# Re-ordering attention and batching the border columns in a scheduled two-layer backbone step on eight cores

## The chip, the cores and the metric

One Trainium2 chip, eight cores, one launch. The metric is the device time of the slowest core in microseconds. Each core works on its own data; the cores do not talk to each other. Executions come in two states: in the slow one, the cores of one die (0 to 3 or 4 to 7) have a lower granted clock and the time is some per cent longer. Profiles are of the slowest core, unless another core is named.

## The reference, cut to what matters

```python
D_MODEL = 1024; D_FF = 2816; SEQ = 256; DEC_SEQ = 2048; PAST_LEN = 512; N_HEADS = 8; N_KV_HEADS = 2

def dwconv3(x, w):                     # centred, width 3, over positions
    xp = jnp.pad(x, ((0, 0), (1, 1), (0, 0)))
    return xp[:, :-2] * w[0] + xp[:, 1:-1] * w[1] + xp[:, 2:] * w[2]

def short_conv_mixer(u, w_in, conv_k, w_out):
    b_gate, c_gate, xp = jnp.split(u @ w_in, 3, axis=-1)
    return (b_gate * dwconv3(c_gate * xp, conv_k)) @ w_out

def conv_ffn(u, w_up, conv_k, w_down):
    h = dwconv3(u @ w_up, conv_k)
    g, up = jnp.split(h, 2, axis=-1)
    return (jax.nn.silu(g) * up) @ w_down

for i in range(2):                     # for context (prompt) and latent tokens
    u = modulate_norm(h, norm_mix_pre[i], s1, sc1)
    y = short_conv_mixer(u, ...) if i == 0 else attention(u, ...)   # latents: rotary q/k, cached + own keys
    h = gated_residual(h, y, norm_mix_post[i], g1)                  # h + gate * rms_norm(y)
    u = modulate_norm(h, norm_ffn_pre[i], s2, sc2)
    h = gated_residual(h, conv_ffn(u, ...), norm_ffn_post[i], g2)
# ... the six modulation vectors come from silu(c) @ mod_w[i]; the prompt's new k, v are outputs too
```

Each core has one latent sequence of 2,048 tokens and four prompts of 256. The kernel cuts this into three units of 1,024 tokens: S0 and S1 (the halves of the latent sequence) and P (the four prompts).

## The kernel before

The program is not written in execution order. Every operation is registered with what it reads and writes; a list scheduler then simulates the engines with modelled durations and fixes one static order for each engine. Priorities are planned TensorE times. An operation that others depend on takes over their urgency; a DMA is wanted 12 us ahead of its first reader:

```python
for o in reversed(self.ops):
    for s in o.succ:
        o.prio = min(o.prio, s.prio - (12.0 if o.nbytes else 1.3 * o.lat))
```

Weights pass through a ring of 23 blocks of 1 KB in each partition. One channel of a ConvFFN's up-projection takes four blocks, so five channels fit; a block of the modulation weights takes four blocks as well:

```python
def load_w(src, cols, after=()):
    nb = (cols * 2 + 1023) // 1024
    if wpos["b"] + nb > wpos["lim"]:
        wpos["b"] = 0
    b = wpos["b"]
    wpos["b"] += nb
    # ...
    P.dma("pool", ap, src, cols * 2 * 128, reads=after, writes=keys)
```

The width-3 convolution needs the neighbour's column at the border of S0 and S1. Before each layer part, S0 gets that one column of S1's normed input (`uh`) and multiplies it with every weight tile ("halo" matmuls of one column). Later S1 reuses a saved column of S0. The result goes into the channel by a one-column VectorE update (`edge`), in the middle of the channel's own chain:

```python
def ffn_in(U, l, ub):                  # cut
    for c in range(NCF):               # 22 channels
        w, wk = load_w(wup[l, c], KC * 256)
        for s in range(2):
            b = nextset()
            o = ((c % 2) * 2 + s) * 1024
            r, rk = ev_t[:, o:o + 1024], A("ev", o * 4, o * 4 + 4096)
            zmm(b, ub, ..., wk, halo=s if U is S0 else None)   # L581, and L588: the halo
            z = z2(b)
            P.act(1024, ..., r, z, AF.Copy, scale=fck(1, s, c))
            if U is S0:
                edge(r, 1023, bank(7, 1, s), fck(2, s, c), ...)            # L610
            if U is S1:
                edge(r, 0, zc, fck(0, s, c), ...)                          # L610
            taps(U, r, z, fck(0, s, c), fck(2, s, c), ...)                 # L606, two per half
        # ... Silu, product into ra
```

`ev_t` is also where an output phase keeps its result until the residual has been added. The order of the stages is: three convolutions (S0, S1, P); FFN-0 (S0, S1, P); S0's and S1's projections; S0's attention; S1's; the prompt's projections and attention; FFN-1 (S0, S1, P). The residual h of two units stays on the chip; h is spilled and reloaded around every stage (72 stores and 72 loads of 512 KB).

Of the kernel before, what the change touches and what calls it, by code (L numbers as in the profile page):

```python
# [13 lines left out]
KC = 8  # L14
DFF = 2816
NCF = 22
# [23 lines left out]
class Prog:  # L40
# [75 lines left out]
    def schedule(self):  # L116
# [11 lines left out]
        for o in reversed(self.ops):  # L128
            for s in o.succ:
                o.prio = min(o.prio, s.prio - (12.0 if o.nbytes else 1.3 * o.lat))  # L130
        order = []
        n = len(self.ops)
        eps = 0.05
        while len(order) < n:
# [51 lines left out]
            for s in o.succ:  # L186
                lag = 0.0 if (s.eng == e == "pe") else 0.06
                s.ready = max(s.ready, (o.t0 + o.busy if s.eng == e == "pe" else o.t1) + lag)
                s.ndep -= 1
                if s.ndep == 0:  # L190
                    heapq.heappush(future[s.eng], (s.ready, s.idx))
# [55 lines left out]
def build_program():  # L247
# [26 lines left out]
    h_mem = nc.dram_tensor("h_mem", [128, KC, TT], F32, kind="Internal").ap()  # L274

    with ExitStack() as es:
# [25 lines left out]
        hc2_t = sb("hc2", 8 * 2 + 4, F32)  # L302
        hsq_t = sb("hsq", 8, BF16)
        uh_t = sb("uh", 8, BF16)
        zs_t = sb("zs", 44, F32)
        ps = es.enter_context(nc.psum_tensor("ps", [128, 4096], F32))[:]
# [25 lines left out]
        first = {"w": ()}  # L332
# [80 lines left out]
        class UBuf:  # L413

            def __init__(self, name, base, ap):
                self.name, self.base, self.ap = name, base, ap.rearrange("p (k t) -> p k t", k=KC)

# [7 lines left out]
        UK = UBuf("ra", 16384, ra_t[:, 8192:16384])  # L425

# [36 lines left out]
        def norm(U, l, ai, bpart, ub, bk=5, allpool=False):  # L463
            mv, cf = mvs[l], cfs[l]
            for ct in range(2):
# [13 lines left out]
                for kc in range(KC):  # L479
                    t = tm_t[:, (kc % 2) * 512:(kc % 2) * 512 + 512]  # L480
                    tk = [("tm", kc % 2)]
                    P.dve(lambda e, kc=kc, t=t, rs=rs, src=hap(U, kc, ct * 512, ct * 512 + 512): e.scalar_tensor_tensor(  # L482
                        out=t, in0=src, scalar=cf[:, ai, kc, U.v:U.v + 1], in1=rs,
                        op0=ALU.mult, op1=ALU.mult), 512, hk(U, kc, ct) + [("rs", ct), ("coef", l, ai, U.v)], tk)
                    P.dve(lambda e, kc=kc, t=t, ct=ct: e.tensor_scalar_add(
                        out=ub.ap[:, kc, ct * 512:ct * 512 + 512], in0=t, scalar1=mv[:, bpart * 8 + kc, U.v:U.v + 1]), 256,
                        tk + [("mod", l, bpart, U.v)], ub.keys(kc, ct * 512, ct * 512 + 512))

        def save_hcol():
            src = h_t[S1.slot].rearrange("p (k t) -> p k t", k=KC)[:, :, 0]  # L490
            P.dve(lambda e: e.tensor_copy(out=hcol_t, in_=src), 60, [k for kc in range(KC) for k in hk(S1, kc, 0)], [("hcol",)])

        def norm_halo(l, ai, bpart):
# [3 lines left out]
            ss, th = hc2_t[:, 16:17], hc2_t[:, 0:8]  # L497
# [9 lines left out]
        def out_phase(U, l, gi, nk, wsrc, rhs_fn, rkeys, ybs, banks, split=False):  # L507
# [4 lines left out]
            order = [(m, ct) for ct in range(2) for m in range(KC)] if split else [(m, ct) for m in range(KC) for ct in range(2)]  # L512

            def finish(ct):
                yb, ybn = ybs[ct]
                rs = rs_t[:, (2 + ct) * 512:(3 + ct) * 512]
                rk = [("rs", 2 + ct)]
                rstd_ops(6 + ct, 512, D, rs, rk)
                for m in range(KC):
                    y = yb[:, m * 512:(m + 1) * 512]  # L520
                    yk = A(ybn, m * 2048, m * 2048 + 2048)
                    P.dve(lambda e, y=y, m=m, rs=rs: e.scalar_tensor_tensor(  # L522
                        out=y, in0=y, scalar=cf[:, gi, m, U.v:U.v + 1], in1=rs, op0=ALU.mult, op1=ALU.mult), 512,
# [3 lines left out]
                    if split and ct == 1 and m % 2 == 0:  # L527
# [6 lines left out]
                    elif ct == 1:  # L534
                        store_h(U, m)

            for m, ct in order:
                yb, ybn = ybs[ct]
                if split or ct == 0:
                    w, wk = load_w(wsrc(m), nk * 128)  # L540
# [11 lines left out]
                y = yb[:, m * 512:(m + 1) * 512]  # L552
                yk = A(ybn, m * 2048, m * 2048 + 2048)
# [12 lines left out]
            if U is S1:  # L566
                save_hcol()
# [9 lines left out]
        def zmm(b, ub, lhs_fn, wk, halo=None):  # L577
# [7 lines left out]
            if halo is not None:  # L585
# [4 lines left out]
                P.pe(fh, 0.35, wk + [("uh",)], pk(7))  # L590
# [18 lines left out]
        def edge(r, col, zc, w, rd, wr):  # L609
            P.dve(lambda e: e.scalar_tensor_tensor(out=r[:, col:col + 1], in0=zc, scalar=w, in1=r[:, col:col + 1],  # L610
                                                   op0=ALU.mult, op1=ALU.add), 30, rd + wr, wr)

        def conv_in(U, ub):
            ck = lambda j, i: par[:, P_CK + j * 8 + i:P_CK + j * 8 + i + 1]
            for i in range(8):
                w, wk = load_w(win[i], KC * 384, after=first["w"])
                first["w"] = ()
                w3 = w.rearrange("p (k n) -> p k n", n=384)
                o = (i % 2) * 2048
                csb, ckk = ev_t[:, o:o + 1024], A("ev", o * 4, o * 4 + 4096)  # L620
                r, rk = ev_t[:, o + 1024:o + 2048], A("ev", o * 4 + 4096, o * 4 + 8192)
                bC = nextset()
                zmm(bC, ub, lambda kc, w3=w3: w3[:, kc, 128:256], wk, halo=0 if U is S0 else None)
                hc = hc2_t[:, 8 + i:9 + i]
                P.act(1024, "ps", pk(bC, bC + 1), ckk, csb, z2(bC), AF.Copy)
                if U is S0:
                    P.act(1, "ps", pk(7), [("hc", i)], hc, bank(7, 1, 0), AF.Copy)
                bX = nextset()
                zmm(bX, ub, lambda kc, w3=w3: w3[:, kc, 256:384], wk, halo=1 if U is S0 else None)
                P.dve(lambda e, csb=csb, bX=bX: e.tensor_tensor(out=csb, in0=csb, in1=z2(bX), op=ALU.mult), 1024,  # L630
                      pk(bX, bX + 1) + ckk, ckk)
                if U is S0:
                    P.dve(lambda e, hc=hc: e.tensor_tensor(out=hc, in0=hc, in1=bank(7, 1, 1), op=ALU.mult), 30,
                          pk(7) + [("hc", i)], [("hc", i)])
# [4 lines left out]
                if U is S0:  # L639
                    edge(r, 1023, hc, ck(2, i), [("hc", i), ("par",)], rk)  # L640
                    P.pool(lambda e, csb=csb, i=i: e.tensor_copy(out=zs_t[:, i:i + 1], in_=csb[:, 1023:1024]), 1, ckk, [("zs", i)])
                if U is S1:
                    edge(r, 0, zs_t[:, i:i + 1], ck(0, i), [("zs", i), ("par",)], rk)
                P.dve(lambda e, r=r, bB=bB, i=i: e.tensor_tensor(out=a3(i, 0, 1024), in0=r, in1=z2(bB), op=ALU.mult), 1024,
                      rk + pk(bB, bB + 1), a3k(i, 0, 1024))
                cur["k"] = a3k(i, 0, 1)
                yield

        def ffn_in(U, l, ub):
            fck = lambda j, s, c: par[:, P_FCK + l * 132 + j * 44 + s * 22 + c: P_FCK + l * 132 + j * 44 + s * 22 + c + 1]  # L650
            for c in range(NCF):
                w, wk = load_w(wup[l, c], KC * 256)
                w3 = w.rearrange("p (k n) -> p k n", n=256)
                rr = []
                for s in range(2):
                    b = nextset()
                    o = ((c % 2) * 2 + s) * 1024
                    r, rk = ev_t[:, o:o + 1024], A("ev", o * 4, o * 4 + 4096)
                    rr.append((r, rk))
                    zc = zs_t[:, c * 2 + s:c * 2 + s + 1]  # L660
                    zmm(b, ub, lambda kc, w3=w3, s=s: w3[:, kc, s * 128:(s + 1) * 128], wk, halo=s if U is S0 else None)
                    z = z2(b)
                    P.act(1024, "ps", pk(b, b + 1) + [("par",)], rk, r, z, AF.Copy, scale=fck(1, s, c))
                    if U is S0:
                        edge(r, 1023, bank(7, 1, s), fck(2, s, c), pk(7) + [("par",)], rk)
                    if U is S1:
                        edge(r, 0, zc, fck(0, s, c), [("zs", c * 2 + s), ("par",)], rk)
                    taps(U, r, z, fck(0, s, c), fck(2, s, c), pk(b, b + 1) + [("par",)], rk)
                    if U is S0:
                        P.act(1, "ps", pk(b + 1), [("zs", c * 2 + s)], zc, z[:, 1023:1024], AF.Copy)  # L670
                (rg, rgk), (ru, ruk) = rr
                P.act(1024, "sb", rgk, rgk, rg, rg, AF.Silu)
                P.pool(lambda e, rg=rg, ru=ru, c=c: e.tensor_tensor(out=a3(c, 0, 1024), in0=rg, in1=ru, op=ALU.mult), 1024,  # L673
                       rgk + ruk, a3k(c, 0, 1024))
                cur["k"] = a3k(c, 0, 1)
                yield

# [4 lines left out]
        ktp = ra_t[:, 18 * 1024:20 * 1024].rearrange("p (j s) -> p j s", j=2)  # L682
        vbp = ra_t[:, 20 * 1024:22 * 1024].rearrange("p (c n) -> p c n", n=256)
# [8 lines left out]
        def ktpk(j, s0, s1):  # L692
            return A("ra", 18 * 2048 + j * 2048 + s0 * 2, 18 * 2048 + j * 2048 + s1 * 2)

        def vbpk(c):
            return A("ra", 20 * 2048 + c * 512, 20 * 2048 + c * 512 + 512)
        TA = A("ra", 18 * 2048, 22 * 2048)
# [4 lines left out]
        bkc = {"i": 0, "s": 0}  # L702

        def nextbank():
            bkc["i"] = (bkc["i"] + 1) % 6
            return bkc["i"]

        def attn_in(U, ub, qbuf):
            if U.sample:
                for a in range(2):  # L710
                    P.dma("sp", tab[:, a, :], rope[a, :, U.ui * 1024:U.ui * 1024 + 1024], 128 * 4096, writes=TA)
            def vpart():
                w, wk = load_w(wv, KC * 256)
                w3 = w.rearrange("p (k n) -> p k n", n=256)
                for tt in range(8):
                    b = nextbank()
# [354 lines left out]
```

## Time and profile before

| | before |
|---|---|
| median of 4 runs | 2938.38 us (2933.79 to 2942.33) |
| profiled span, slowest core | 2933.4 us |
| mean granted TensorE clock | 0.956 (cores 0.954 to 0.957) |

In the profile's lines PE is TensorE, PEld its weight loads, DVE VectorE, ACT ScalarE, POOL GpSimd (which also issues the weight loads' DMAs) and SP SyncE; L581 is line 581 of the kernel that the lines are of. The page of before, its first lines (busy time of each engine, its share of the span, instructions):

```profile
span 2933.4 us, 38857 instructions; the slowest of 8 cores (2922.7 to 2933.4 us)
...
PE 2589.0 (88%) x13935; PEld 1177.7 (40%) x13935; DVE 1512.6 (52%) x1650; ACT 1299.8 (44%) x1712; POOL 1001.4 (34%) x851
```

TensorE is the engine to look at: 88% busy, and the next is at 52%. But busy time is not necessary time. The Trainium skill, "Perfetto Trace Analysis", section "Identifying the Most-Contended Engine", says that the matmul busy share is a poor measure of the distance to the limit, because matmuls are pipelined. The trace agrees: 560 back-to-back matmuls of 128x512 took 121.03 us, 216 ns each, while their group on the profile's page has a mean of 391 ns for one. With 216 ns for each of the 10,524 matmuls of 512 columns, and the start-to-start times of the smaller ones, I get 2,452 us of necessary TensorE time. The remaining 481 us are "lost": waits, and matmuls at a lowered clock. I use this word below, stage by stage: length minus necessary time.

TensorE's waits in before (who waits, for what: total us, times, longest us):

```profile
PE ps L588 <- DVE ev L610: 34.6, 24, 10.7
PE ps L581 <- DVE ev L606: 29.0, 21, 5.8
...
PE ps L581 <- DMA wr<-win: 23.2, 7, 6.1
PE ps L581 <- DVE ev L610: 19.3, 6, 6.8
```

The longest row: a halo matmul (L588) waits for a one-column update (L610). That update is itself queued on VectorE, as the chain at the start of FFN-0's first unit shows (before; start us, duration us, what):

```profile
513.57 5.53 DVE ev L522 x5
...
519.92 3.42 DVE ev L522 x2
523.34 0.13 DVE ev L610
...
523.52 1.41 issue
524.93 1.27 DVE ev L606
```

L522 is the residual of the previous stage, which works in `ev`. The first `edge` comes after it on VectorE, 0.13 us of work after 9 us of residual.

That is only the start. Of the 22.2 us that halo matmuls wait in this unit, 16.2 lie after 555 us, in 18 waits of at most 1.2 us. All halo matmuls write one bank of PSUM, the matmul's result memory, and each waits until the `edge` of the one before has read it (before, TensorE's timeline, about the same every 15 us):

```profile
573.15 0.34 PE L588 MATMUL ps<-uh,wr 128*128 128x1 bf16 x8
573.97 0.34 PE L588 MATMUL ps<-uh,wr 128*128 128x1 bf16 x8 [0.47 <-DVE ev L610]
575.48 0.34 PE L588 MATMUL ps<-uh,wr 128*128 128x1 bf16 x8 [1.18 <-DVE ev L610]
576.74 10.52 PE L581 MATMUL ps<-u,wr 128*128 128x512 bf16 x48 [0.92 <-DVE ev L606]
```

### The profile page before, as it was taken

What the parts mean: (1) busy time and instruction counts of PE and PEld (TensorE: products, weight loads), DVE (VectorE), ACT (ScalarE), POOL (GpSimd) and SP (SyncE); (2) the same over time, 40 slices, a digit from 0 to 9 for tenths busy, and PEclk for the clock granted to TensorE, in tenths of its full rate; (3) what the DMA queues carried; (4) which work ended last, traced back from release to release, by engine and by line L of the source; (5) the groups of instructions that cost most, each with busy time, mean ns of one, the idle gap of its engine ahead of it and who ended that gap; (6) DMA issues with size and microseconds to landing.
All of it is one profiled execution on the core that took longest, in us unless ns stands there. A gap on an engine that the chain in (4) does not pass through costs nothing.

```text
span 2933.4 us, 38857 instructions; the slowest of 8 cores (2922.7 to 2933.4 us)
## 1 busy us (share of the span) xinstructions
PE 2589.0 (88%) x13935; PEld 1177.7 (40%) x13935; DVE 1512.6 (52%) x1650; ACT 1299.8 (44%) x1712; POOL 1001.4 (34%) x851
## 2 busy tenths in 40 slices
PE   2898888888989799997689998997879999999996
PEld 1443333333434344443244443442434443444442
DVE  3456463754379708715441214424387629846743
ACT  2241324333334325423448867875544425433432
POOL 1133241532254416415861005004154416425422
PEclk9999998988999999998899999999999999999998
DMA  8646666443457346743740013006345446536456
GB/s 219 132 70 129 130 140 116 115 94 78 74 104 145 69 85 144 129 83 72 189 88 5 1 26 119 1 15 169 58 109 105 83 83 139 110 71 129 79 90 133
DMA packets 85740, 288.31 MB, mean 98 GB/s; under 512 B 10416, under 2 KB 11952, under 8 KB 84528
## 3 DMA queue, kind: packets, MB, share of 16 engines
q0 software_dynamic: 48368, 171.99, 35.2%
q1 hardware_dynamic: 37184, 113.83, 12.1%
q8 instruction: 116, 1.90, 0.3%
q14 instruction: 72, 0.59, 0.1%
HBM read 405.32 MB, written 52.43 MB: 156 GB/s over the span
## 4 chain that ended last, share of the span: by engine, by line
PE 70%; DVE 10%; issue 7%; DMA 6%; ACT 3%; POOL 1%; SPq 1%; DVEq 0%; ACTq 0%; POOLq 0%
PE ps L581 32%; PE ps L549 20%; PE ps L829 5%; PE ps L821 5%; DVE ev L522 3%; DVE ev L606 3%; PE ps L755 2%; PE ps L838 1%; DMA wr<-win 1%; DMA h<-x_in 1%; PE ps L855 1%; PE ps L773 1%; DVE yb L522 1%; DMA yb<-modw 1%; PE ps L558 1%
## 5 line engine op out<-in xcount | busy, mean ns | idle before, releaser
L581 PE MATMUL ps<-u,wr 128*128 128x512 bf16 x5376 | 1237.0, 391 | 95.5 <-DVE ev L606 29.0
L581 PEld LDWEIGHTS ps<-u,wr 128*128 128x128 bf16 x5376 | 529.9, 100 | 757.0 <-issue 181.0
L606 DVE SCALAR_TENSOR_TENSOR ev<-ps,par,ev 128x1023 f32<-128x1023 f32 (+1 forms) x528 | 671.4, 1279 | 91.9 <-ACT ev L100 56.0
L549 PE MATMUL ps<-ra,wr 128*128 128x512 bf16 x2752 | 622.5, 382 | 22.2 <-DVE ev L606 12.6
L100 ACT ACTIVATE ev<-ps,par 128x1024 f32<-128x1024 f32 x264 | 293.6, 1112 | 394.5 <-PE ps L581 351.1
L673 POOL TENSOR_TENSOR ra<-ev 128x1024 bf16<-128x1024 f32 x132 | 318.2, 2411 | 355.5 <-DVE ev L606 248.5
L549 PEld LDWEIGHTS ps<-ra,wr 128*128 128x128 bf16 x2752 | 269.6, 98 | 354.1 <-issue 36.9
L100 ACT ACTIVATE wr<-ps 128x1024 bf16<-128x1024 f32 x336 | 327.1, 1022 | 60.6 <-PE ps L821 56.9
L522 DVE SCALAR_TENSOR_TENSOR ev<-ev,coef,rs 128x512 f32<-128x512 f32 x96 | 145.6, 1571 | 367.7 <-ACT rs L100 367.7
L482 DVE SCALAR_TENSOR_TENSOR tm<-h,coef,rs 128x512 f32<-128x512 f32 x192 | 149.3, 815 | 149.1 <-ACT rs L100 149.1
L100 ACT ACTIVATE ev<-ps 128x512 f32<-128x512 f32 (+2 forms) x128 | 84.8, 663 | 309.3 <-PE ps L549 224.7
L100 ACT ACTIVATE sqb<-ps 128x512 bf16<-128x512 f32 x252 | 146.4, 599 | 94.4 <-PE ps L755 85.2
L829 PE MATMUL ps<-wr,ra 128*128 128x512 bf16 x672 | 186.2, 381 | 0.5 <-DVE ra L845 0.3
L473 POOL TENSOR_TENSOR sqa<-h 128x512 bf16<-128x512 f32 x104 | 114.6, 1117 | 165.6 <-DMA h<-x_in 72.7
L526 POOL TENSOR_TENSOR h<-h,yb 128x512 f32<-128x512 f32 x92 | 135.9, 1491 | 97.1 <-DVE yb L522 96.0
L113 POOL DMA_DIRECT2D wr<-wup x132 | 75.6, 574 | 268.8 <-PE ps L558 118.9
L100 ACT ACTIVATE ev<-ev 128x1024 f32<-128x1024 f32 x132 | 138.9, 1052 | 59.9 <-DVE ev L606 59.3
L526 POOL TENSOR_TENSOR h<-h,ev 128x512 f32<-128x512 f32 x96 | 146.6, 1554 | 38.7 <-DVE ev L522 38.6
L100 ACT ACTIVATE yb<-ps 128x512 f32<-128x512 f32 x96 | 57.4, 598 | 207.8 <-PE ps L549 206.1
L113 POOL DMA_DIRECT2D wr<-wo x24 | 13.0, 541 | 379.7 <-PE ps L549 331.4
L522 DVE SCALAR_TENSOR_TENSOR yb<-yb,coef,rs 128x512 f32<-128x512 f32 x96 | 111.3, 1186 | 56.1 <-ACT rs L100 56.0
L113 POOL DMA_DIRECT2D wr<-wdn x56 | 31.2, 557 | 273.5 <-PE ps L558 128.2
(102 smaller groups left out, 2048.9 us busy)
## 6 DMA issues: line engine op xcount, KB each, us to landing
wr<-wup POOLq DMA_DIRECT2D x132, 512.0 KB, 6.4
wr<-wdn POOLq DMA_DIRECT2D x56, 704.0 KB, 7.1
h_mem<-h SPq DMA_DIRECT2D x72, 512.0 KB, 6.9
h<-h_mem SPq DMA_DIRECT2D x72, 512.0 KB, 5.4
wr<-modw POOLq DMA_DIRECT2D x40, 512.0 KB, 7.4
wr<-win POOLq DMA_DIRECT2D x24, 768.0 KB, 10.2
h_out<-h SPq DMA_DIRECT2D x48, 256.0 KB, 3.0
h<-x_in SPq DMA_DIRECT2D x16, 512.0 KB, 11.2
```

Source lines behind the costliest of these rows:

```text
L100: return self._add("act", lambda e: e.activation(out=out, in_=in_, func=func, **kw), reads, writes, busy, busy + 0.12, table=self.TABLES.g ...
L113: return self._add(q, lambda e: e.dma_start(out=out, in_=in_, **kw), reads, writes, 0.55 if q == "pool" else 0.65, 0.0, nbytes=nbytes, rat ...
L473: P.pool(lambda e, s=s, src=src: e.tensor_tensor(out=s, in0=src, in1=src, op=ALU.mult), 512, hk(U, kc, ct), [("sqa", i)])
L482: P.dve(lambda e, kc=kc, t=t, rs=rs, src=hap(U, kc, ct * 512, ct * 512 + 512): e.scalar_tensor_tensor(out=t, in0=src, scalar=cf[:, ai, kc, ...
L522: P.dve(lambda e, y=y, m=m, rs=rs: e.scalar_tensor_tensor(out=y, in0=y, scalar=cf[:, gi, m, U.v:U.v + 1], in1=rs, op0=ALU.mult, op1=ALU.mu ...
L526: fa = lambda e, y=y, hh=hh: e.tensor_tensor(out=hh, in0=hh, in1=y, op=ALU.add)
L549: ins = e.matmul(bank(b), w3[:, k, :], rhs_fn(k, ct), start=(k == 0), stop=(k == nk - 1))
L581: ins = e.matmul(bank(b + ct), lhs_fn(kc), ub.ap[:, kc, ct * 512:ct * 512 + 512], start=(kc == 0), stop=(kc == KC - 1))
L606: P.dve(lambda e, ro=ro, zi=zi, w=w: e.scalar_tensor_tensor(out=ro, in0=zi, scalar=w, in1=ro, op0=ALU.mult, op1=ALU.add), 1024, rd + wr, wr)
L673: P.pool(lambda e, rg=rg, ru=ru, c=c: e.tensor_tensor(out=a3(c, 0, 1024), in0=rg, in1=ru, op=ALU.mult), 1024, rgk + ruk, a3k(c, 0, 1024))
L821: ins = e.matmul(o, K[:, j, k0:k0 + 128], rhs, start=True, stop=True)
L829: ins = e.matmul(bank(4 + a), V[:, c, j * 128:(j + 1) * 128], pt[:, a * 512:(a + 1) * 512], start=(ki == 0), stop=(ki == nk - 1))
```

## The change

Its intent is to take out what TensorE waits for at the borders of stages: batch the border columns, keep the first channels out of the residual's buffer, spill less, and mix projections (which wait for short chains on other engines) with attention (which has many matmuls ready). The core of the diff, cut:

```diff
@@ scheduler
+            own = o.prio
             for s in o.succ:
                 o.prio = min(o.prio, s.prio - (12.0 if o.nbytes else 1.3 * o.lat))
+            if o.eng == "pe":
+                o.prio = max(o.prio, own - 6.0)
...
-                lag = 0.0 if (s.eng == e == "pe") else 0.06
+                lag = 0.0 if (s.eng == e == "pe") else (0.7 if s.eng == "pe" and not o.nbytes else 0.06)
@@ zmm
-            if halo is not None:
+            if halo is not None and ub.halo:
...
-                P.pe(fh, 0.35, wk + [("uh",)], pk(7))
+                at(P.prio + late, lambda: P.pe(fh, 0.35, wk + [("uh",)], pk(7)), False)
@@ conv_in
-                csb, ckk = ev_t[:, o:o + 1024], ...
+                csb, ckk = raf[:, o:o + 1024], ...          # a part of ra
@@ ffn_in
+                zt, zn, o2 = (raf, "ra", 7168 + (c % 2) * 2048) if c < 8 else (ev_t, "ev", (c % 2) * 2048)
-                    zmm(b, ub, ..., halo=s if U is S0 else None)
+                    zmm(b, ub, ..., halo=s * 22 + c, late=18.0)
-                    if U is S0:
-                        edge(r, 1023, bank(7, 1, s), fck(2, s, c), pk(7) + [("par",)], rk)
-                    if U is S1:
-                        edge(r, 0, zc, fck(0, s, c), [("zs", c * 2 + s), ("par",)], rk)
+            if col is not None:                             # after all 22 channels: 44 columns at once
+                P.dve(... out=e2_t, in0=zh, in1=par[:, q0:q0 + 44], op=ALU.mult ...)
+                P.dve(... out=e2v, in0=e2v, in1=ev2, op=ALU.add ...)
+                P.act(22, "sb", ..., e2_t[:, 0:22], e2_t[:, 0:22], AF.Silu)
+                P.dve(... out=dst, in0=e2_t[:, 0:22], in1=e2_t[:, 22:44], op=ALU.mult ...)
@@ order of stages (convolutions unchanged, modulation blocks moved)
+        stage(ffn_in(S1, 0, UU, True), ffn_out(S1, 0, spill=True), ...)     # FFN-0 now S1, P, S0
+        stage(ffn_in(PU, 0, UU, False), ffn_out(PU, 0), ...)
+        stage(ffn_in(S0, 0, UU, False), ffn_out(S0, 0, YS), ..., (mod_gen(1, [3, 4]), 4, 1.6))
+        run(qkv(PU, UU, UQ, KV + Q, True, [0, 1, 2, 3], [4, 5], 4))
+        weave(qkv(S0, UE, UU, ...), (attend(PU, UQ, ...), 0, 0.85))
+        # ... the prompt's output; u of S1 comes back from DRAM
+        g = attend(S0, UU, [(yb_t, "yb", 12288)])
+        steps(g, 12)
+        run(qkv(S1, UQ, None, KV, True, [0, 1, 2, 3], [7], 3))
+        weave(g, (qkv(S1, UQ, UE, Q, False, [7], [7], 3, evac=True), 1, 8.5))
+        # ... S1's attention, outputs
+        stage(ffn_in(S0, 1, UU, True), ..., (mod_gen(1, [5]), 4, 3.0))
```

`late=18.0` plans a halo matmul 18 us after its channel, as nobody needs its result before the end of the unit. The new lines in the scheduler ("the floor") keep a TensorE operation from becoming more than 6 us more urgent than its own plan. `qkv` is new and runs its steps two items deep as a pipeline. Spills fall from 72 stores and 72 loads to 24 and 24.

## The prediction

> **What bounds it now.** TensorE. In the timeline 560 back-to-back 128x512 matmuls take 121.03 us: 216 ns each. The program has 10,524 matmuls of 512 columns (groups of instructions), 2,273 us at that pace; with fp32 passes, 256-column and tiny ones at their start-to-start times I get 2,452 us of necessary TensorE time in a span of 2,933. Both kernels have the same 13,799 matmuls, so the change can only win from the other 481 us. By stage (start-to-start minus necessary, from the timeline):
>
> - before the first conv: 60
> - conv projections: 20, 32, 28
> - FFN-0 projections: S0 65, S1 19, prompt 10; their output phases 25
> - attention (two projections, attend, output, prompt): 143, of which S0's projection 52 and the prompt 39
> - FFN-1: 22, 12, 9; last output phase 31
>
> About 360 are visible waits, 115 cold clock after them. The Trainium skill, "TensorE: Matmul & The Clock Gate", Part 1, says an idle window of about 3.4 us halves the clock; this trace agrees (records of 3.4 us at 0.5, granted mean 0.956; dense stretches at 1.00).
>
> **Removed.** (1) Border columns: 192 one-column VectorE updates (554 ns SBUF, 212 ns PSUM, 74 us in all) and the halo matmuls' wait on them (34.6 us, the largest in the table of waits) become a few batched operations. FFN-0 S0 should fall near the others' 10 to 19: minus 50; FFN-1 S0 minus 10; conv minus 7. (2) Conv and the first 8 FFN channels leave `ev`, so a stage's start no longer waits for the previous residual (chain of waits: VectorE `ev` L522, 3.2%): minus 4 to 8 at each of six starts, about 35. (3) Spills and reloads of h drop from 72 to 24 each, 48 MB of 288: fewer weight waits in conv (23 us now), but the first conv takes 8 instead of 4 modulation blocks; minus 10 net. (4) Attention: prompt first, software-pipelined, S0's and S1's projections among attention matmuls. S0's attention with S1's queries needs about 218 us TensorE and 184 ScalarE, so TensorE stays the limit. Prompt attention with S0's projections needs about 86 us TensorE but 83 ScalarE (16 jobs x 2.6 us, 20 items x 1.9), so I allow stalls there. Excess 143 to about 65: minus 78.
>
> **Added.** 24 small DMAs for u of S1, 16 VectorE evacuations of 0.7 us, 16 POOL squares of 1.1 us, small border copies: off the path, on engines busy 34 to 52%.
>
> **Not touched.** The start (60) and the tail (31).
>
> **Sum.** 481 - 67 - 35 - 10 - 78 = 291; 2,452 + 291 = 2,743 in the profile; about 8 us more in the unprofiled median, as before: 2,750, range 2,690 to 2,830. Faster 0.95, same 0.04, slower 0.01.
>
> **What would show it.** TensorE busy up from 88% to about 94%, granted clock from 0.956 to about 0.975; FFN-0's first unit as short as its others plus 9 us of halo matmuls; no wait on one-column VectorE updates; the attention block 740 us instead of 806; start and last output phase unchanged.
>
> **What would make it wrong.** The static order assumes engine times; if ScalarE or VectorE are slower than it assumes, TensorE queues behind one late instruction and each stall cools the clock (2,830). Prompt attention with one-bank sets may be bound by latency through ScalarE. VectorE still has residual, norm and taps together at each FFN start, so (2) may give nothing. Or the freed DMA and PSUM hide more than I count (2,690).

## More of the kernel before

Only fast runs are compared here.

An operation that overwrites a buffer depends on that buffer's readers. So a weight load is a successor of the matmuls that still read the old weights in its place.

## The result

| | before | after |
|---|---|---|
| median of 4 runs | 2938.38 us (2933.79 to 2942.33) | 2775.28 us (2771.87 to 2776.17) |
| profiled span | 2933.4 us | 2773.4 us |
| granted clock, profiled core | 0.956 | 0.976 (others 0.977 to 0.982) |

The ratio is 0.9443, with a 95% interval of 0.9424 to 0.9463. A ratio is always the mean time of one kernel's fast runs over that of the other's of the same rounds, so not quite the ratio of the medians.

The page of after, the same lines:

```profile
span 2773.4 us, 38402 instructions; the slowest of 8 cores (2744.9 to 2773.4 us)
...
PE 2549.2 (92%) x13935; PEld 1167.3 (42%) x13935; DVE 1466.2 (53%) x1497; ACT 1303.9 (47%) x1739; POOL 1021.2 (37%) x971
```

Busy TensorE time fell by 40 us although the matmuls are the same: fewer of them ran at the lowered clock (start-to-start times of 420 to 440 ns between matmuls of 512 columns: 293 in before, 178 in after). The Trainium skill, "TensorE: Matmul & The Clock Gate", Part 1, section "What's actually happening", says that an idle window of about 3.4 us takes the clock to a half. The traces' clock records agree in length and value: all are at 1 or 0.5, in steps of about 3.4 us, 260.7 us at 0.5 in before and 135.9 in after. But the window need not be idle throughout: between 555 and 735 us of before the clock fell ten times, and no wait of TensorE there is longer than 1.2 us. Half clock costs at most half of its time, so up to about 62 of the 160 us that the change gained are time at a lowered clock; that is an estimate from the two sums.

Where the time came from, by the same accounting (lost us, profiled core; a group's lines sum to it):

| stage | before | after | change |
|---|---|---|---|
| start, to the first projection | 60 | 62 | +2 |
| conv projections, 1st / 2nd / 3rd unit | 20 / 32 / 29 | 26 / 12 / 11 | -32 |
| FFN-0 projections, 1st / 2nd / 3rd | 65 / 19 / 10 | 28 / 13 / 5 | -48 |
| FFN-0 outputs | 15 | 2 | -12 |
| attention block | 152 (of 808) | 94 (of 743) | -58 |
| FFN-1 projections, 1st / 2nd / 3rd | 23 / 12 / 9 | 27 / 8 / 2 | -7 |
| FFN-1 outputs, mostly the last | 32 | 26 | -5 |
| all (with 4 at the conv outputs in both) | 481 | 321 | -160 |

The first unit of each FFN, the one with the halo matmuls, stands out: 28 and 27 lost, where the last units lose 5 and 2.

TensorE's waits in after (L606 is the projection matmul now, L613 the halo matmul, L631 the taps):

```profile
PE ps L606 <- DVE ra L631: 23.4, 20, 3.7
PE ps L606 <- DMA wr<-win: 18.8, 6, 4.9
PE ps L606 <- DMA wr<-wup: 17.9, 5, 4.7
```

The waits on one-column updates are gone. A row is new: projections wait 17.9 us for the up-projection's weights (`wup`). It lies in the two first units: 9.1 and 8.8 us there. The chain of waits in FFN-0's first unit of after shows how such a wait comes about:

```profile
545.70 0.40 PE ps L384 x16
546.10 0.41 PE ps L613 x16
546.52 0.02 issue
546.54 0.02 POOLq L212
546.56 0.23 issue
546.79 5.08 DMA wr<-wup
551.87 0.14 issue
552.01 8.20 PE ps L606 x26
```

Read it downward: halo matmuls (L613) end, 0.3 us later the load queue issues a weight load, this lands 5.08 us later, and 0.14 us after that the projection starts. So the load was released by the halo matmul, and TensorE waited for it. The timeline of the issuing engine in after shows what else is odd (start us, duration us; the loads alone):

```profile
537.22 0.59 POOL L113 DMA_DIRECT2D wr<-modw  x1 [0.84 <-PE ps L613]
...
546.79 1.13 POOL L113 DMA_DIRECT2D wr<-wup  x2
547.90 0.55 POOL L113 DMA_DIRECT2D wr<-modw  x1
548.42 1.09 POOL L113 DMA_DIRECT2D wr<-wup  x2
```

No load for almost 10 us, then five in under 3 us. In the same stretch of the TensorE timeline the halo matmuls come in bursts, up to 16 at a time. A halo matmul is the last reader of its channel's weights. Planned 18 us late, it holds the channel's four blocks of the ring.

That is the theory for the first FFN units: **late halo matmuls keep weights in the ring, and the loads that need the place come late and in bursts**. The rival: the FFN's first units carry modulation blocks woven in; these take ring places too and collide with the weights, and the batching itself is fine.

In the attention block, the prediction expected stalls where the prompt's attention is woven with S0's projections. The table of stretches of after (stretch, length, then busy us of each engine with counts, clock, DMA share, GB/s):

```profile
1256.00:1330.00 74.00, 60.16 (x272) 26.60 (x270) 55.91 (x74) 45.37 (x80) 43.45 (x45) 0.91 0.41 81
1330.00:1430.00 100.00, 96.66 (x468) 49.08 (x466) 46.67 (x67) 71.05 (x146) 45.88 (x46) 1.00 0.27 49
...
1470.00:1510.00 40.00, 29.78 (x172) 14.47 (x173) 26.34 (x20) 17.50 (x27) 29.41 (x21) 0.83 0.67 213
1510.00:1750.00 240.00, 235.77 (x1585) 108.86 (x1585) 68.51 (x84) 182.70 (x202) 68.45 (x60) 1.00 0.09 16
```

The second row is that stretch, and it is dense: 96.66 of 100 us, clock 1.00. So is the last, S0's attention with S1's queries. The losses are where a projection is not woven with attention: the prompt's own (first row, clock 0.91) and S1's keys and values (third row, clock 0.83).

### The profile page after: what moved, and what is told of

The parts are those of the page before. It is cut to its first block, busy times and chain, and to the rows that moved or that the text cites. A ratio compares the mean times of both kernels' runs of the same rounds, so it can differ in the third digit from the quotient of the medians.

```text
span 2773.4 us, 38402 instructions; the slowest of 8 cores (2744.9 to 2773.4 us)
## 1 busy us (share of the span) xinstructions
PE 2549.2 (92%) x13935; PEld 1167.3 (42%) x13935; DVE 1466.2 (53%) x1497; ACT 1303.9 (47%) x1739; POOL 1021.2 (37%) x971
## 4 chain that ended last, share of the span: by engine, by line
PE 74%; DVE 8%; DMA 7%; issue 7%; ACT 3%; POOL 1%; SPq 1%; DVEq 0%; ACTq 0%; POOLq 0%
PE ps L606 30%; PE ps L576 22%; PE ps L915 5%; PE ps L923 5%; DVE ra L631 3%; PE ps L795 3%; DMA wr<-win 2%; PE ps L932 2%; PE ps L957 2%; PE ps L585 1%; PE ps L826 1%; PE ps L484 1%; DMA yb<-modw 1%; DMA wr<-wup 1%; DVE yb L549 1%
## 5 line engine op out<-in xcount | busy, mean ns | idle before, releaser
L606 PE MATMUL ps<-u,wr 128*128 128x512 bf16 x5376 | 1208.3, 385 | 85.3 <-DVE ra L631 23.4
L606 PEld LDWEIGHTS ps<-u,wr 128*128 128x128 bf16 x5376 | 525.7, 99 | 734.8 <-issue 140.1
L631 DVE SCALAR_TENSOR_TENSOR ev<-ps,par,ev 128x1023 f32<-128x1023 f32 (+1 forms) x336 | 427.8, 1280 | 194.6 <-ACT ev L100 162.4
L100 ACT ACTIVATE wr<-ps 128x1024 bf16<-128x1024 f32 (+1 forms) x352 | 333.6, 984 | 98.8 <-PE ps L915 96.1
L100 ACT ACTIVATE ev<-ps,par 128x1024 f32<-128x1024 f32 x168 | 186.8, 1112 | 278.8 <-PE ps L606 276.4
L712 POOL TENSOR_TENSOR ra<-ev 128x1023 bf16<-128x1023 f32 (+1 forms) x84 | 199.8, 2379 | 146.9 <-DVE ev L631 66.5
L631 DVE SCALAR_TENSOR_TENSOR ra<-ps,par,ra 128x1023 f32<-128x1023 f32 (+1 forms) x192 | 239.0, 1272 | 21.4 <-ACT ra L100 12.2
L549 DVE SCALAR_TENSOR_TENSOR ev<-ev,coef,rs 128x512 f32<-128x512 f32 x80 | 110.3, 1409 | 178.6 <-ACT rs L100 178.6
L100 ACT ACTIVATE ra<-ps,par 128x1024 f32<-128x1024 f32 x96 | 106.4, 1110 | 102.9 <-PE ps L606 69.4
L553 POOL TENSOR_TENSOR h<-h,ev 128x512 f32<-128x512 f32 x80 | 114.3, 1443 | 37.9 <-DVE ev L549 37.4
L712 POOL TENSOR_TENSOR ra<-ra 128x1023 bf16<-128x1023 f32 (+1 forms) x48 | 115.8, 2412 | 30.3 <-ACT ra L100 18.7
L100 ACT ACTIVATE ev<-ps 128x512 f32<-128x512 f32 x80 | 47.6, 596 | 167.4 <-PE ps L576 163.7
```

The costliest lines, as they stand in the source:

```text
L100: return self._add("act", lambda e: e.activation(out=out, in_=in_, func=func, **kw), reads, writes, busy, busy + 0.12, table=self.TABLES.g ...
L549: P.dve(lambda e, y=y, m=m, rs=rs: e.scalar_tensor_tensor(out=y, in0=y, scalar=cf[:, gi, m, U.v:U.v + 1], in1=rs, op0=ALU.mult, op1=ALU.mu ...
L553: fa = lambda e, y=y, hh=hh: e.tensor_tensor(out=hh, in0=hh, in1=y, op=ALU.add)
L606: ins = e.matmul(bank(b + ct), lhs_fn(kc), ub.ap[:, kc, ct * 512:ct * 512 + 512], start=(kc == 0), stop=(kc == KC - 1))
L631: P.dve(lambda e, ro=ro, zi=zi, w=w: e.scalar_tensor_tensor(out=ro, in0=zi, scalar=w, in1=ro, op0=ALU.mult, op1=ALU.add), 1024, rd + wr, wr)
L712: P.pool(lambda e, rg=rg, ru=ru, c=c: e.tensor_tensor(out=a3(c, c0, c1), in0=rg[:, c0:c1], in1=ru[:, c0:c1], op=ALU.mult), 1024, rgk + ruk ...
```

## The experiments

Twelve runs in three batches, each batch on one chip: the first four, the next four, the last four. All gave correct results. All differ from the changed kernel as their diff shows. The changed kernel itself was timed again as a control in the second batch (2773.8 us), and e9, which puts stores back, took 2773.9 in the third; that chips agree within about 2 us is read from this, if e9's stores cost nothing, and from the kernel before, which took 2938.2 in the first comparison and 2936.7 and 2938.4 in the second and third batch. There was no control in the first batch. The ratios of the first batch are about half a per cent too low: seven runs of the kernel before on that chip count as fast, but range from 2930 to 2959 us, most with some cores at a clock of 0.945, and average 2951.2, against 2936.7 and 2938.4 in the other batches. So I compare mean fast times with 2773.8, and give ratios beside them.

| kernel | fast runs | mean us | ratio to before (95%) | against 2773.8 |
|---|---|---|---|---|
| halo at once (e1) | 4 | 2717.0 | 0.9207 (0.917 to 0.9243) | -57 |
| modulation moved (e2) | 4 | 2766.2 | 0.9373 (0.9337 to 0.9409) | -8 |
| edge for each channel (e3) | 4 | 2741.9 | 0.9296 (0.9253 to 0.9339) | -32 |
| `ev` back (e4) | 2 | 2799.0 | 0.9484 (0.9425 to 0.9544) | +25 |
| control (e5) | 2 | 2773.8 | 0.9445 (0.9326 to 0.9565) | |
| halo 6 us late (e6) | 2 | 2722.9 | 0.9272 (0.9163 to 0.9381) | -51 |
| attention not woven (e7) | 3 | 2813.6 | 0.9581 (0.9475 to 0.9687) | +40 |
| old scheduler rules (e8) | 3 | 2734.3 | 0.9306 (0.9197 to 0.9415) | -40 |
| all spills (e9) | 4 | 2773.9 | 0.9442 (0.9386 to 0.9497) | 0 |
| floor removed (e10) | 3 | 2736.8 | 0.9312 (0.9258 to 0.9366) | -37 |
| e1 with e8 (e11) | 6 | 2733.0 | 0.9299 (0.926 to 0.9339) | -41 |
| e1, modulation even (e12) | 6 | 2716.4 | 0.9243 (0.9209 to 0.9277) | -57 |

### e1: halo matmuls at once

```diff
-                    zmm(b, ub, ..., wk, halo=s * 22 + c, late=18.0)
+                    zmm(b, ub, ..., wk, halo=s * 22 + c, late=0.0)
```

> Halo matmuls of the FFN's first units issued right behind their channel instead of 18 us later, nothing else. In the changed kernel the first FFN units still waste 28 and 27 us, of which 9.1 and 8.8 us are TensorE waits on up-projection weights. Theory A: a halo matmul that comes 18 us late keeps its channel's weight buffer occupied for another 2 to 3 channels, so the next weight loads are issued too late; with late = 0 the weight waits of both first units fall under 4 us each and the time falls by 8 to 20 us, to about 2757 to 2767. Rival B: the modulation blocks that share the weight ring and the queue in these two stages (8 blocks and 4 blocks) are what makes the loads late; then nothing changes: 2770 to 2780 and the weight waits stay at 7 to 10 us each. Rival C: the halo matmuls at once wait for the halo column's norm instead and it gets slower by up to 10 us.

Measured: 2717.0 us, 57 under the changed kernel. The theory had the direction and the place right, and its size far too low. The profile fell in the slow state (die 0 at 0.960 to 0.970), so I read core 5, on the undisturbed die: span 2712.8, clock 0.984. Its FFN-0 first unit loses 0.8 us (28.3 in after), FFN-1's 4.8 (27.1); every other stage is within 5 us. The chain in that unit, e1, core 5:

```profile
526.14 3.48 PE ps L606 x16
529.62 0.18 PE ps L613 x8
529.79 3.48 PE ps L606 x16
533.27 0.18 PE ps L613 x8
```

Projections and halo matmuls alternate, with no load in the chain, and TensorE's only wait in the whole unit is 0.4 us. Why was the size off? I counted the 17.9 us of waits on `wup`. The two units lost 50 us more in after than in e1. Shorter waits of other names are in it, and time at a lowered clock: 17.4 of the first unit's 28.3 lost us are waits that the trace shows, 10.9 are not. The clock's records fit: 23.9 and 20.5 us at 0.5 in the two units of after, none in those of e1.

### e2: modulation blocks out of FFN-1's first unit

```diff
-              (mod_gen(1, [3, 4]), 4, 1.6))
+              (mod_gen(1, [3, 4, 5]), 2, 1.2))
-        stage(ffn_in(S0, 1, UU, True), ..., (mod_gen(1, [5]), 4, 3.0))
+        stage(ffn_in(S0, 1, UU, True), ...)
```

> The last four modulation blocks are loaded in FFN-0's S0 stage instead of in FFN-1's first unit; halo matmuls stay 18 us late. Theory A (late halo matmuls hold the weight ring): FFN-1's first unit keeps at least 6 us of weight waits and the time stays within 6 us of the changed kernel. Rival B (modulation blocks crowd the ring): its weight waits fall under 3 us and the time falls by 6 to 15 us.

Measured: 2766.2, 8 us faster (the control's two runs are 11 us apart, so the stage says more than the total). FFN-1's first unit loses 16.3 instead of 27.1; FFN-0's, which kept its blocks, 29.5 as before. Waits in FFN-1's first unit, e2:

```profile
PE ps L606 <- DVE ra L631: 9.3, 3, 3.7
...
PE ps L606 <- DMA wr<-wup: 0.3, 1, 0.3
```

So the rival has a part: without modulation blocks, in this unit, the ring has slack enough that the late halo matmuls no longer delay a load (0.3 us in place of 8.8). It takes both, lateness and full ring, for a late load; taking either away helps, and the lateness is the larger part, as e1 shows with all modulation blocks in place.

### e3: a border update for each channel, as before the change

```diff
-                    zmm(..., late=18.0)
+                    zmm(..., late=0.0)
+                    if col is not None:
+                        edge(r, col, ..., wj, ..., rk)          # one column, on each channel half
-            if col is not None:                                 # no batch at the end of the unit
+            if False:
```

The Silu and the product take the full width again. The convolution keeps its batch.

> Border columns of the FFN done channel by channel again, as in the kernel before: one-column VectorE update per half channel, halo matmuls at once, full-width Silu and product. To be compared with e1_late0, which differs in the batching alone. The prediction's term for this was 60 us (50 in FFN-0, 10 in FFN-1). If the term is right: 2757 + 60 = about 2815, with a TensorE wait on the one-column updates of 25 us or more back in the table. Rival: the 65 us lost in FFN-0's first unit before were owed mostly to the ev buffer and the order of work, not to the columns: then under 20 us slower than e1.

Measured: 2741.9. That is 25 us slower than e1, from which it differs by the batch alone, and 32 faster than the changed kernel. So the batching is worth 25 us, 9 and 12 of them in the two first FFN units, but as it was shipped, with late halo matmuls, the border part of the change cost more than it gave. FFN-0's first unit loses 9.9 us here, not before's 65.3, though its per-channel updates are back. TensorE's waits in that unit, e3 (its L635 is the `edge`):

```profile
PE ps L606 <- DVE ra L635: 4.9, 4, 1.8
...
PE ps L613 <- DVE ev L635: 0.5, 1, 0.5
PE ps L613 <- DVE ra L635: 0.3, 1, 0.3
```

The halo matmul's wait on a one-column update, 22.2 us in before's first FFN-0 unit, is 0.8 here. So most of that wait was not the one-column updates' own cost, and it came back neither through the updates nor through the shared PSUM bank, which e3 has too. What else of the change removed it was not separated: FFN-0's first unit is S1 instead of S0, its first channels lie outside `ev`, and the scheduler is another. (With the batch in place, neither of the last two brings the loss back: 32.3 us with `ev`, e4, against 28.3; 2.1 with the old scheduler rules, e8.)

### e4: conv and the first FFN channels back in `ev`

```diff
-                o = 4096 + (i % 2) * 2048
-                csb, ckk = raf[:, o:o + 1024], A("ra", ...)
-                r, rk = raf[:, o + 1024:o + 2048], A("ra", ...)
+                o = (i % 2) * 2048
+                csb, ckk = ev_t[:, o:o + 1024], A("ev", ...)
+                r, rk = ev_t[:, o + 1024:o + 2048], A("ev", ...)
...
-                zt, zn, o2 = (raf, "ra", 7168 + (c % 2) * 2048) if c < 8 else (ev_t, "ev", (c % 2) * 2048)
+                zt, zn, o2 = ev_t, "ev", (c % 2) * 2048
```

> Convolution results of the conv stages and of the first 8 FFN channels written to ev again, as before, nothing else. The prediction's term: 35 us, 4 to 8 us at each of six stage starts, as projections wait again for the residual that still reads ev: 2775 + 35 = about 2810, with TensorE waits on ScalarE or VectorE work on ev at the stage starts. Rival: VectorE has residual, norm and taps at each stage start anyway and is the limit there, so the buffer matters little: under 10 us.

Measured: 2799.0, 25 us slower than the control, from two fast runs that lie 12 us apart. Lost: conv's second unit 22.4 (12.0), FFN-0's first 32.3 (28.3), second 22.6 (12.5), FFN-1's third 10.8 (1.9); others within 5 us. In two of the four the step is the one predicted: FFN-0's second and FFN-1's third unit each lose 9.2 us in their first 20 us, where the changed kernel loses 0.1. The longest wait, of FFN-1's third unit, e4 (L631 are the taps):

```profile
PE ps L606 <- DVE ev L631: 8.9, 1, 8.9
```

FFN-0's first unit loses 3.7 more at its start. Conv's second unit does not fit: it loses 0.1 us in its first 20 in both kernels and the 10 us later on, with 7.9 us instead of 4.5 of waits for its weights (`win`). Why is not shown. So writing to `ev` costs 4 to 9 us at three starts (predicted: 4 to 8 at six), and the 25 us are not all of that kind.

### e5: the changed kernel again

No edit; the control of the second batch.

> The changed kernel again, unedited, as the control on the chip of these runs: 2770 to 2780 in the fast state if the chip is like the first, and the ratio 0.94 to the kernel before.

Measured: 2773.8 from two fast runs (2768.2 and 2779.5). The second of them is not quite undisturbed: cores 6 and 7 have 147 us at a granted clock of 0.8125. The mean still agrees with the four runs of the result (2774.6).

### e6: halo matmuls 6 us late

```diff
-                    zmm(..., late=18.0)
+                    zmm(..., late=6.0)
```

> Halo matmuls 6 us late instead of 18. If the ring is the mechanism there is a threshold: the ring holds five channels of 7 us each, so holding a slot one channel longer still lets a load be issued some 20 us ahead of its use: within 6 us of e1_late0 (ratio to before 0.919 to 0.924), first FFN units with under 4 us of weight waits. If instead every microsecond of lateness costs (more weight switches, late border work), a third of the 60 us comes back: 20 us slower than e1_late0 (ratio about 0.927).

Measured: 2722.9, 51 us under the control on the same chip and within 6 us of e1. So the cost does not grow in proportion to the lateness; a small one is nearly free. A ring of places with slack would act like this: nothing until the slack is used up. But e10 below gives a second reason, and this run does not tell the two apart. Two fast runs only. The slowest core's trace lacks matmul records; core 3's is whole (2717.7 us, clock 0.985), and its first FFN units lose about 4 and 10 us, with no wait for `wup` in either. (The ratio alone would have pointed elsewhere; it has another batch's denominator than e1's.)

### e7: attention without the weaving

```diff
-        weave(qkv(S0, UE, UU, KV + Q, True, [3, 4], [5, 7], 3), (attend(PU, UQ, ...), 0, 0.85))
+        run(attend(PU, UQ, ...))
+        run(qkv(S0, UE, UU, KV + Q, True, [0, 1, 2, 3], [4, 5], 3))
-        steps(g, 12)
-        run(qkv(S1, UQ, None, KV, True, [0, 1, 2, 3], [7], 3))
-        weave(g, (qkv(S1, UQ, UE, Q, False, [7], [7], 3, evac=True), 1, 8.5))
+        run(qkv(S1, UQ, UE, KV + Q, True, [0, 1, 2, 3], [4, 5], 3))
+        run(g)
```

> Prompt attention still first, but nothing woven: prompt attention runs before S0's projections, S1's projections all run before S0's attention, with four main and two auxiliary PSUM banks and ScalarE evacuation. The attention block of the changed kernel is 743 us with 94 lost. If weaving earns the attention gain: the block grows back to 790 to 810 us, the time to about 2825 to 2840. Rival: the software pipelining of the projections by two items is what earned it, and weaving little: the block within 15 us of 743.

Measured: 2813.6, 40 us slower than the control; but the three fast runs are 2801.8, 2810.6 and 2828.6, and in the last the cores of die 1 have a clock of 0.960 to 0.967. Without it the mean is 2806.2, 32 slower. The profile is of the run of 2801.8. The attention block takes 779.1 us and loses 130.4, against 743.0 and 94.3 woven, and 808.0 and 151.9 before. So the weaving is worth about 36 us of the 58, and the rest of the rewrite (the prompt first, the pipeline two items deep) about 22, each from one profile. The edit also changes what weaving made necessary: the projections get four main PSUM banks instead of two (S0) or one (S1's queries), and S1's queries are copied out by ScalarE. Neither part alone explains the gain.

### e8: the old scheduler rules

```diff
-            if o.eng == "pe":
-                o.prio = max(o.prio, own - 6.0)
-                lag = 0.0 if (s.eng == e == "pe") else (0.7 if s.eng == "pe" and not o.nbytes else 0.06)
+                lag = 0.0 if (s.eng == e == "pe") else 0.06
```

> The two rules of the list scheduler as before (no floor under an inherited TensorE priority, 0.06 instead of 0.7 us assumed from another engine to TensorE), the rest as changed. The diff's title does not name them. If they matter, TensorE's order is built on results that come later than assumed and short waits of 0.3 to 0.7 us multiply: 10 to 40 us slower. Rival: within 6 us, as the order of the large matmuls hardly moves.

Measured: 2734.3, 40 us *faster* than the control. It is the opposite of what I had expected. FFN-0's first unit loses 2.1 us here and FFN-1's 10.9, with `late=18.0` still in place. Worse became mainly the convolution's second unit (24.1, from 12.0) and FFN-1's second output phase (8.0, from almost none); the convolution's first unit got better (15.3, from 25.8).

### e9: all spills back

```diff
-        stage(conv_in(S1, UU, False), conv_out(S1), ...)
+        stage(conv_in(S1, UU, False), conv_out(S1, spill=True), ...)
```

and the same for five more output phases: 48 stores of 512 KB again, without the loads.

> The changed kernel with 48 stores of h put back (every unit is stored after every layer half, 72 in all as before), 25 MB more of writes; the loads are not put back. The prediction booked 10 us for spills and modulation blocks together. If DMA traffic is off the path: within 6 us of the control, 2765 to 2785. If it delays the weight loads: conv projections of units 2 and 3 lose 12 and 11 us in the changed kernel and would lose 5 to 10 us more each, 2785 to 2800.

Measured: 2773.9, the control's time. The stores are off the critical path. The 48 loads that the change also removed were not tested.

### e10: the floor alone removed

```diff
-            if o.eng == "pe":
-                o.prio = max(o.prio, own - 6.0)
```

> Only the floor under an inherited TensorE priority is taken out; halo matmuls still 18 us late by their own priority, 0.7 us assumed lag kept. e8_old_sched was some 40 us faster than the changed kernel. Theory: the weight load that waits for a halo matmul hands its urgency back to it (12 us ahead of its own use), and the floor of 6 us cuts that off, so floor and lateness only hurt together: then this run is 30 us or more faster than the changed kernel, 2730 to 2745, with the first FFN units losing under 12 us each. Rival: it was the assumed lag: then it stays at 2765 to 2785.

Measured: 2736.8, 37 us under the control; so nearly all that e8 gained is the floor. FFN-0's first unit loses 4.9 and FFN-1's 7.6; as in e8, conv's second unit (17.6) and FFN-1's second output phase (7.4) lose more. All the waits of TensorE in the first of them, e10 (the lines are two up, L604 is the projection):

```profile
PE ps L604 <- DVE ra L629: 1.4, 2, 1.0
PE ps L482 <- ACT rs L100: 1.2, 1, 1.2
PE ps L604 <- ACT zs L100: 1.1, 2, 0.5
```

No wait for weights, with `late=18.0`. The reading: a weight load is wanted 12 us before its first use, and hands this urgency back to everything it depends on, so also to the halo matmul whose weights it overwrites. Without the floor, a halo matmul planned 18 us late is thus pulled forward when a load needs its place. The floor allows 6 us of that and no more, so 12 us of the planned lateness stay; with `late=6.0` (e6) none stays.

The kept traces show this in the loads (worked out from issue, landing and start times). From the sixth channel on, the time from the issue of a channel's weights to their first use is never under 10.1 us in e10's two first units. In after it goes from 5.2 to 30.7 us, and three loads, issued 5.2, 7.2 and 5.4 us ahead, land 0.1 to 0.2 us before their use: TensorE waited for them. But it is not that halo matmuls run earlier in general without the floor. Counted in the order of channels, they start on average 14.2 us behind their channel in e10's FFN-1 unit and 10.7 us in after's, and yet e10 loses 7.6 us there and after 27.1. What counts is not how late they are on average, but whether the one whose place a load wants is done in time.

### e11: e1 and the old scheduler rules

```diff
-                    zmm(..., late=18.0)
+                    zmm(..., late=0.0)
```

and the diff of e8.

> Halo matmuls at once and both scheduler rules as before. If the rules only hurt by way of the halo matmuls: like e1_late0 or slower by up to 15 us, since e8_old_sched lost 10 us more in the second conv unit and 8 us in the last but one output phase (ratio 0.921 to 0.926). If the new rules hurt elsewhere too: faster than e1_late0, ratio under 0.919.

Measured: 2733.0 from six fast runs, 16 us slower than e1, and the same as e8. (One of the six, 2745.5, has up to 250 us at a clock of 0.8125 on die 1; without it, 2730.5, 14 slower.) So the new rules are worth about 14 to 16 us where they do no harm, and with the old rules it does not matter how late the halo matmuls are planned, as those that a load waits for are pulled forward anyway.

### e12: e1 with the modulation blocks spread more evenly over the convolution

```diff
-              (mod_gen(0, [2, 3]), 1, 0.8), ...     # beside conv S0
+              (mod_gen(0, [2]), 2, 1.0), ...
-              (mod_gen(0, [4]), 2, 1.0), ...        # beside conv S1
+              (mod_gen(0, [3, 4]), 1, 0.8), ...
```

> Halo matmuls at once, and the modulation blocks spread 4, 8, 4 over the three conv units instead of 8, 4, 4. The first conv unit loses 24 to 26 us in the changed kernel against 20 before, with 13 to 19 us of waits on conv weights, which I put down to the four more blocks in its stage. If so, it falls to 15 to 20 us and the second rises by less: 3 to 8 us faster than e1_late0, ratio 0.918 to 0.920. Rival: those waits come from the loads of h and the first weights, and nothing moves.

Measured: 2716.4, no different from e1 (2717.0). On core 5 conv's first unit loses 16.2 (24.2 in e1) and the second 15.2 (11.8): the weight waits moved with the blocks. A miss, and no better version. The best kernel is e1, or e12 equally: 2.1% faster than the changed kernel.

## Why the prediction was right, and where it was wrong

The class was right, and the time of 2775.28 us lies within the range, 25 us over the point. The frame held: TensorE bounds both kernels, 2,452 us are necessary in both, and only the 481 lost us can change. They fell to 321, not to 291. Term by term:

**Term 1, the border columns (predicted 67: 50 in FFN-0's first unit, 10 in FFN-1's, 7 in conv). This is the step that failed.** Measured: 37 less in FFN-0's first unit, 4 *more* in FFN-1's, 6 more in conv's first (where the change also put four more modulation blocks; e12 moved them and conv's first unit lost 8 us less). I listed the halo matmuls as something that only stops waiting, and put no price on *when* they run. The runs show that price. Planned 18 us late, and kept there by the floor, they hold weights in the ring, and the loads behind them arrive late (5.08 us for one in the chain of after). Taking out the lateness is worth 51 to 57 us (e6, e1), taking out the floor 37 (e10). In e1 the first FFN units lose 64 and 18 us less than before: there, my 50 and 10 would have been too low. The reason, the one-column updates, is only a part of it: with the updates back and the halo matmuls on time, FFN-0's first unit still loses only 9.9 (e3), and the batch is worth 25 us in all. Which part of the change took FFN-0's first unit from 65 to 10 without the batch is not settled.

**Term 2, out of `ev` (predicted 35).** Right in kind, smaller in size: 25 us by e4, of which only FFN-0's second and FFN-1's third unit show the predicted wait in full; 10 us in conv's second unit are of another, unknown kind.

**Term 3, less DMA traffic (predicted 10).** The stores are worth nothing (e9). The conv units had 23.2 us of waits for `win` in before and have 18.8 in after; e12 shows these waits moving with the modulation blocks. The loads were not tested.

**Term 4, attention (predicted 78).** 58 measured. The block takes 743 us, as against 740, but from a base of 808 and not 806, and some of my 78 was counted against a smaller loss (143, where this accounting has 152). Weaving is about 36, the rest 22 (e7). The place where I allowed stalls was wrong: the woven stretch is dense, and the unwoven projections at its two ends lose.

**Not in the sum.** FFN-0's output phases gave 12 us and FFN-1's 5. I left both out.

**The signs.** The clock (0.976 on the profiled core), the attention block, the start, and the lack of waits on one-column updates came as stated. TensorE's busy share came to 92%, not 94. FFN-0's first unit took 193.9 us, where its second took 170.9: the sign "as short as its others plus 9 us" failed, and pointed straight at the step that was wrong. In e1 it takes 165.7. The last output phase shrank by 8 us; I had said unchanged.

So the prediction was close by luck, because errors met: the late halo matmuls spoiled the border term, while that term without them, and the output phases, give more than I counted. Without the lateness the kernel would have been at 2717, under my point.

## What to carry to other kernels

An operation whose result nobody needs soon may still be urgent, if it is the last reader of a buffer that a load wants: in a ring, a plan that puts off the reader puts off the load. When a change batches small work to the end of a stage, ask what each piece holds while it waits, and look in the chain of waits for a load that starts right after a small operation. And when a scheduler gets a rule that limits inherited urgency, check what depended on the inheritance before giving anything a late plan.

## What the Trainium skill lacked or had wrong

- No page I used says that the last reader of a weight buffer sets when the next load into it can be issued, and that a late reader turns into a wait for a DMA. In these runs, halo matmuls of 0.18 us for eight, planned late, led to 17.9 us of visible waits for weights and to 51 to 57 us of time (after against e6 and e1). A load of 512 KB took 5.08 us from issue to landing in that chain.
- "TensorE: Matmul & The Clock Gate", Part 1, section "Seeing it yourself", says that a die is held at 13/16 of the clock once three of its cores run dense matmuls, while the load lasts. Here all eight cores ran dense matmuls with random data, and in the profiled runs of before and after no core has a record at 13/16; a 128x512 matmul took 216 ns in a dense stretch. The value itself does occur (records of 0.8125): in e1's slow profile on all four cores of die 0, 252 to 363 us each, but also for a while in two runs that count as fast, the control's (147 us, on cores 6 and 7 only) and e11's (97 to 250 us, on die 1). One slow run of the kernel before took 3303.31 us with die 1 at means of 0.807 to 0.815. So it happens in some executions, for part of their time and not always on the whole die.
- Same page, Part 1, section "What's actually happening": the half clock after an idle window of about 3.4 us agrees with the trace in length and value, but a window need not be idle throughout: in before's first FFN-0 unit the clock fell ten times between 555 and 735 us, where no wait is longer than 1.2 us. The price in a kernel with many short waits: in after's first FFN-0 unit 17.4 us of waits went with 10.9 us of further loss.
- "Perfetto Trace Analysis", section "Identifying the Most-Contended Engine", was right about the matmul busy share. The busy share of weight loads, one of the two measures that it advises instead, does not show the distance by itself either: it was 40% and 42%, where the necessary share of the span was 83.6% and 88.4% (2,452 over 2,933.4 and over 2,773.4).
